# Start of a one-core transformer block: inputs laid out in tile order, shift, scale and first GLU products block by block

## The chip, the cores and the metric

The kernel runs on one core of a Trainium2 chip. TensorE (PE) multiplies matrices and loads its stationary operand beside that (PEld), VectorE (DVE) and ScalarE (ACT) work on whole tiles, GpSimd (POOL) does the same more slowly, and SyncE (SP) issues nearly all DMAs, which 16 DMA engines carry out. The metric is the device time of one execution in microseconds. Host work that prepares the inputs is outside it, in both kernels.

## The reference, cut to what matters

The block takes 256 latent tokens `x` and 256 context tokens `ctx` of 1024 channels and two condition vectors `c` and `c_ctx`. It begins so:

```python
mod_lat = silu(c)     @ w_ada + b_ada        # 6 x 1024 columns: shift, scale, gate, twice
mod_ctx = silu(c_ctx) @ w_ada + b_ada
u_ctx = h_ctx * (1 + csc_m) + csh_m          # per channel
u_lat = h_lat * (1 + sc_m) + sh_m
q, k, v, g, glu, gates = split(u_lat @ w_in + b_in)      # w_in: 1024 x 10240
k_c, v_c = split(u_ctx @ w_in[:, K_OFF:G_OFF] + b_in[K_OFF:G_OFF])
za, zb = split(glu); z = za * sigmoid(zb)    # then a depthwise convolution, 31 taps per channel
```

After that come retention over q, k and v, the convolution branch, two gated output projections, a layer norm, a router that picks two of 32 experts per token, the experts' SwiGLU products (6 MB of float32 weights each) and a second layer norm.

## The kernel before

All of it is one program on one core, in float32. The products of the mixing stage are made three times at reduced precision: each operand is split into a high and a low part, and `mm3` (line 96) adds high by high, high by low and low by high. The split of a weight slice (128 x 1024) is one copy on ACT and one subtraction on VectorE (`Slice.emit`, lines 163 and 164); that of the input is in `modulate` (line 293), per block of 128 channels: the high part on ACT, the full value and the low part on VectorE.

What comes first is written out by hand. Lines 371 to 387 load `w_ada` in pieces of 512 rows x 512 columns (`ada_load`, 1 MB each, rows of 2 KB), multiply them with the condition vectors (`ada_half`), copy the sums out (`ada_row`), and transpose them into columns of shift and scale (`ada_mod`). Column block 2 (scale) comes first and block 0 (shift) second; these two cover channels 0 to 511. Between them the program loads parameters as rows of 128 numbers and turns them into columns by PE transposes (`load_cond`, `params`, `more_params`), and transposes x, 16 times 128 x 128 (`transpose_in`, line 284). The decay rates of the retention are computed here as well (`decay_rates`, line 248).

Then `early` (line 483) runs: six clock fillers (`keep_clock`: matmuls whose result nobody reads), the modulation of channels 0 to 511, and GLU products. GLU has four column groups `hb` of 512 columns, and each has four slices `kq` of 256 input channels. `early` does slices 0 and 1 of groups 0 to 2, with column blocks 3 and 1 of `w_ada` between them, and then modulates channels 512 to 1023. Two matmuls with a zero operand open the accumulators of each group (line 435).

The other slices are steps in a list that `run_steps` (line 192) works off: a step emits the splits of up to two later slices (`LEAD`), does its matmuls, its post-processing, and pops `NTAP` operations of the depthwise convolution for VectorE. `ctx` is loaded and transposed on PE, and modulated by steps placed by `CTX`; the sections of `w_ada` that are used later come as side operations from step `SIDE0` on (`ada_rest`, line 784). After the GLU steps come `distances`, the k, q, v and g projections (`proj_k`, line 555, and others), retention, the gates and output projections. A step list sets the order on all engines; SyncE issues loads in program order, each when a buffer of its tag is free (`W8` four, `Y8` six, `Q8` three).

The expert stage (from line 1587) goes through 16 pairs of experts. `load_to` (line 1040) issues each weight tile, 1 MB with rows of 8 KB, as soon as the buffer that `slots` names is free. The `down` weights of the last pair are loaded in column pieces (`load_cols_of`, line 1035).

Of the kernel before, what the change touches and what calls it, by code (L numbers as in the profile page):

```python
# [17 lines left out]
D = 1024  # L18
NT = 256
# [10 lines left out]
SIDE0, SIDE = 4, 9  # L30
NPOS, APOS, TPOS, QPOS, AHEAD = 7, 9, 7, 5, ()
NTAP = (3, 5, 3, 4, 4, 2)
KS0, KS1 = 6, 0
# [4 lines left out]
CTX = 2, 6, 7, 8, 2  # L38
EB = (0, 0), (1, 0), 9
# [6 lines left out]
def tile_block(ctx, tc, a, out):  # L46
# [9 lines left out]
    w_in = a["w_in"][0]  # L56
    w_ada = a["w_ada"][0]
# [187 lines left out]
    for i, nm in enumerate(("ret_decay_fwd", "ret_decay_bwd")):  # L245
        gload(lgx[:, 8 * i:8 * i + 8], bass.AP(tensor=a[nm].tensor, offset=a[nm].offset, ap=[[0, P], [1, 8]]))
# [17 lines left out]
    V.memset(s32, 0.0)  # L264

    def load_cond():
        rows = row1("crow2", (16, P))
        load(rows[0:8], a["c"].rearrange("o (r c) -> (o r) c", c=P))
        load(rows[8:16], a["c_ctx"].rearrange("(r c) -> r c", c=P))
        S.activation(rows, rows, AF.Silu)  # L270
        ps = misc("pps")
        T.transpose(ps[:, 0:16], rows, ident[:16, :16])
        V.tensor_copy(pcol[:, 0:16], ps[:, 0:16])
        V.tensor_copy(s32[:, :, 0], pcol[:, 0:8])
        V.tensor_copy(s32[:, :, 1], pcol[:, 8:16])

    def load_params():
        rows = row1("prow", (48, P))
        load(rows[0:16], a["b_ada"][0, 0:2048].rearrange("(r c) -> r c", c=P))
        for i, nm in enumerate(("conv_dw_b", "conv_ln_g", "conv_ln_b", "b_conv_out")):  # L280
            load(rows[16 + 8 * i:24 + 8 * i], a[nm][0].rearrange("(r c) -> r c", c=P))
        return rows

    def transpose_in(src, dst, name):
        for k2 in range(4):
            ps = misc(f"{name}{k2}", (P, 2, NT))
            for kk in range(2):
                for t in range(2):
                    T.transpose(ps[:, kk, t * P:(t + 1) * P],
                                src[:, t, (2 * k2 + kk) * P:(2 * k2 + kk + 1) * P], ident)  # L290
            S.activation(dst[:, 2 * k2:2 * k2 + 2, :], ps, AF.Copy)
# [12 lines left out]
    def load_tok(name):  # L304
        t = big("Y8", [P, 2, D], f"{name}_t")
        load(t, a[name][0].rearrange("(t p) d -> p t d", p=P))
        return t

# [3 lines left out]
    brow = row1("brow", (80, P))  # L312
    crow = big("Y8", [TAPS, D], "crow")
# [5 lines left out]
    def ada_load(cb, r):  # L319
        adas["w", cb, r] = load_rows(w_ada, 512 * r, 512 * cb, f"wa{cb}_{r}")  # L320

    def ada_half(cb, r):
        if r == 0:
            adas[cb] = acc(f"ada{cb}")
        ps, w = adas[cb], adas["w", cb, r]
        for j in range(4):
            T.matmul(ps[32 * j:32 * j + 32, :], s32[:, 4 * r + j, :], w[:, j, :],
                     start=(r == 0), stop=(r == 1))

    def ada_row(cb):  # L330
        row = adas["r", cb] = sb.tile([P, 512], F32, tag="b2", name=f"adr{cb}", bufs=2)
        S.activation(row, adas[cb], AF.Copy)

    def ada_mod(cb):
        row = adas["r", cb]
        pt = misc(f"adt{cb}", (P, 4, P))
        for c in range(4):
            T.transpose(pt[:, c, :], row[:, c * P:(c + 1) * P], ident)
        m = mod[:, :, 4 * cb:4 * cb + 4]
        V.tensor_reduce(m.rearrange("p r c -> p c r"), pt.rearrange("p c (j r) -> p c r j", r=32)[:, :, 0:2, :],  # L340
                        op=ALU.add, axis=AX.X)
        for r in range(2):
            V.scalar_tensor_tensor(m[:, r], m[:, r], 1.0 if cb >= 2 else 0.0, pcol[:, 16 + 4 * cb:20 + 4 * cb],
                                   op0=ALU.add, op1=ALU.add)

    start = {}

    def load_rest():
        start["p"], start["x"] = load_params(), load_tok("x")

    def params():
        ps = misc("pps2")
        T.transpose(ps[:, 0:48], start["p"], ident[:48, :48])
        V.tensor_copy(pcol[:, 16:64], ps[:, 0:48])

    def load_rest2():
        load(brow, a["b_in"][0].rearrange("(r c) -> r c", c=P))
        load(crow, a["conv_dw"][0])
        transpose_in(start["x"], xT, "xt")

    def more_params(_):
        ps = misc("pbs")
        T.transpose(ps[:, 0:80], brow, ident[:80, :80])
        V.tensor_copy(bcol, ps[:, 0:80])
        ps = misc("pts", (P, 8, 32))
        for k in range(8):
            T.transpose(ps[:, k, 0:TAPS], crow[:, k * P:(k + 1) * P], ident[:TAPS, :TAPS])
        V.tensor_copy(taps, ps[:, :, 0:TAPS])


    ada_load(2, 0)
    load_cond()
    ada_half(2, 0)
    ada_load(2, 1)
    decay_rates()
    load_rest()
    ada_half(2, 1)
    ada_row(2)
    params()
    ada_mod(2)  # L380
    ada_load(0, 0)
    load_rest2()
    ada_half(0, 0)
    ada_load(0, 1)
    ada_half(0, 1)
    ada_row(0)
    ada_mod(0)
# [29 lines left out]
    def load_glu(hb, r):  # L417
        t = big("W8", [P, 4, 512], f"wz{hb}_{r}")
        for h in range(2):
            c0 = GLU_OFF + D * h + 256 * hb  # L420
            load(t[:, :, 256 * h:256 * h + 256],
                 w_in[512 * r:512 * r + 512, c0:c0 + 256].rearrange("(k p) c -> p k c", p=P))
        return t

    gws, gsl, gmm = {}, {}, {}

    def glu(hb):
        ws = gws[hb] = [lazy(load_glu, hb, r) for r in range(2)]
        box = {}

        def mm(kq, q, between=None):
            if kq == 0:
                for i in range(2):
                    box[i] = (misc if hb == 2 else acc)(f"glu{2 * hb + i}", (P, 2, NT))
                    T.matmul(box[i], zero, ulat[0][0:1, 0:2, :], start=True, stop=False)
            for i in range(2):
                for h in range(2):
                    if between and (i, h) in between:
                        between[(i, h)]()
                    cs = slice(256 * h + P * i, 256 * h + P * i + P)  # L440
                    for kk in range(2):
                        k = 2 * kq + kk
                        mm3(box[i][:, h], (q[0][:, kk, cs], q[1][:, kk, cs]), (ulat[0][:, k, :], ulat[1][:, k, :]),
                            False, k == 7 and h == 1)
# [10 lines left out]
        def steps_(kqs):  # L455
            for kq in kqs:
                step(lambda q, kq=kq: mm(kq, q), post if kq == 3 else None, sl[kq], NTAP[0])
                yield

        sl = gsl[hb] = [Slice(lambda kq=kq: ws[kq // 2]()[:, 2 * (kq % 2):2 * (kq % 2) + 2, :], f"qz{hb}_{kq}")  # L460
                        for kq in range(4)]
        gmm[hb] = lambda kq, between=None: mm(kq, sl[kq].q, between)
        return steps_(range(4) if hb > 2 else (2, 3))
# [3 lines left out]
    def ctx_load(_):  # L467
        cbox["t"] = load_tok("ctx")

    def ctx_tr(_):  # L470
        cbox["T"] = big("X8", [P, 8, NT], "cT")
        transpose_in(cbox["t"], cbox["T"], "ct")
# [10 lines left out]
    def early():  # L483
        more_params(None)
        keep_clock(KS0)
        gsl[0][0].emit()
        gws[1][0]()
        ada_load(3, 0)
        ada_load(3, 1)
        modulate(xT, ulat, 0, 0, 4, "um")  # L490
        gsl[0][1].emit()
        gmm[0](0)
        gsl[1][0].emit()
        gws[2][0]()
        gmm[0](1)
        ada_load(1, 0)
        ada_half(3, 0)
        ada_half(3, 1)
        gsl[1][1].emit()
        ada_row(3)  # L500
        ada_load(1, 1)
        gws[0][1]()
        gws[1][1]()
        gmm[1](0)
        ada_mod(3)
        gsl[2][0].emit()
        gmm[1](1)
        gsl[2][1].emit()
        ada_half(1, 0)
        gmm[2](0, {EB[0]: lambda: (ada_half(1, 1), ada_row(1)), EB[1]: lambda: ada_mod(1)})  # L510
        gmm[2](1, {EB[2]: lambda: ada_mod(1)})
        keep_clock(KS1)
        gsl[0][2].emit()
        modulate(xT, ulat, 0, 4, 6, "um")
        modulate(xT, ulat, 0, 6, 8, "um")
# [1180 lines left out]
```

## Time and profile before

| | us |
|---|---|
| median of 3 runs | 996.86 (996.44 to 998.81) |
| the profiled execution, its own time | 1000.41 |
| its span in the profile | 998.6 |
| PE busy | 942.7 |
| VectorE busy | 506.3 |
| ACT busy | 310.2 |
| GpSimd busy | 104.4 |
| DMA moved | 294.81 MB, 295 GB/s on average |

Times in the profile count from the start of the span. A busy PE is not a PE at its peak: matmuls are pipelined, and the clock that the chip grants TensorE has two levels, 1.2 and 2.4 GHz; the profile shows the granted clock as a share, 0.50 or 1.00, with a mean where a window holds both. Up to the first change that the profile records, a window shows 1.00 whatever the clock was. In a row of the timeline the duration runs from the start of the first instruction to the end of the last of those merged into it; one float32 matmul leaves two records.

### The profile page before, as it was taken

The numbers are of one execution on the slowest core, as the hardware profiler recorded it, in microseconds if no ns is written. First come the engines' busy times: TensorE is split into PE (matmuls) and PEld (weight loads), VectorE is DVE, ScalarE is ACT, GpSimd is POOL, SyncE is SP. The second block draws the span as 40 slices with busy tenths as digits, with TensorE's granted clock in tenths as the row PEclk, the third lists the DMA queues.
The fourth block names the chain that finished last, engine by engine and source line by source line (L and its number), as shares of the span: only waits on it lengthen the run. The fifth ranks groups of instructions, "written<-read, shape, count | busy, mean of one in ns | idle before, by whom it ended". The sixth has DMA issues, their size and how long they took to land. (4 is left out here: it accounts for less than half of the span.)

```text
span 998.6 us, 15317 instructions
## 1 busy us (share of the span) xinstructions
PE 942.7 (94%) x6354; PEld 691.5 (69%) x6354; DVE 506.3 (51%) x976; ACT 310.2 (31%) x458; POOL 104.4 (10%) x122
## 2 busy tenths in 40 slices
PE   3999999999999999989989999999999989999884
PEld 2799879779879869889976655656565554655452
DVE  1377988897886996785884111222221111222135
ACT  3357735443543444375443111111110101111010
POOL 1002120210210020721520000000000000000001
PEclk9699999999999999999999999999999998999998
DMA  8795634544374347759986899999999999999991
GB/s 269 231 362 202 220 107 129 214 143 160 115 253 142 136 139 239 268 185 289 348 331 272 346 419 419 421 420 420 420 419 420 421 419 421 421 420 420 421 366 44
DMA packets 92424, 294.81 MB, mean 295 GB/s; under 512 B 6921, under 2 KB 37825, under 8 KB 68288
## 3 DMA queue, kind: packets, MB, share of 16 engines
q1 hardware_dynamic: 91360, 293.31, 76.4%
q0 software_dynamic: 992, 0.49, 0.4%
q8 instruction: 51, 0.84, 0.4%
q14 instruction: 21, 0.17, 0.1%
HBM read 292.71 MB, written 1.06 MB: 294 GB/s over the span
## 5 line engine op out<-in xcount | busy, mean ns | idle before, releaser
L1465 PE MATMUL dn<-wdown,hT 128*64 128x512 f32 (+1 forms) x528 | 120.7, 584 | 6.3 <-DMA wdown<-in_w_exp_down_dram 6.0
L1365 PE MATMUL gu<-wgate,xe 128*64 128x256 f32 x1024 | 122.5, 391 | 2.2 <-DVEq L1625 2.2
L1365 PE MATMUL gu<-wup,xe 128*64 128x256 f32 x1024 | 118.3, 380 | 4.2 <-DMA wup<-in_w_exp_up_dram 4.1
L1371 DVE TENSOR_TENSOR h<-h,gu 128x256 f32<-128x256 f32 x32 | 13.5, 421 | 198.2 <-ACT h L1370 198.2
L404 DVE SCALAR_TENSOR_TENSOR slab<-zp,taps,slab 128x256 f32<-128x256 f32 x232 | 107.1, 515 | 0.0
L1365 PEld LDWEIGHTS gu<-wgate,xe 128*64 128x64 f32 x1024 | 74.5, 141 | 45.8 <-issue 10.3
L1365 PEld LDWEIGHTS gu<-wup,xe 128*64 128x64 f32 x1024 | 74.1, 137 | 42.8 <-DMA wup<-in_w_exp_up_dram 8.2
L1465 PEld LDWEIGHTS dn<-wdown,hT 128*64 128x64 f32 x528 | 37.6, 136 | 76.6 <-issue 59.9
L1370 ACT ACTIVATE h<-gu 128x256 f32<-128x256 f32 x32 | 12.3, 385 | 210.9 <-PE gu L1365 210.8
L1480 DVE SCALAR_TENSOR_TENSOR dl<-dn,ws,ohq 128x512 fp32r<-128x512 f32 x30 | 22.5, 751 | 104.3 <-ACT ohq L1479 104.3
L1479 ACT ACTIVATE ohq<-dn,ws 128x512 fp32r<-128x512 f32 x30 | 20.6, 688 | 125.4 <-PE dn L1465 122.7
L98 PE MATMUL ya<-rT,qro 128*128 128x256 f32 x128 | 36.7, 286 | 2.6 <-DVE rT L750 2.6
L97 PE MATMUL glu<-ulh,qz 128*128 128x256 f32 x128 | 37.5, 293 | 0.0
L99 PE MATMUL ya<-rT,qro 128*128 128x256 f32 x128 | 36.6, 286 | 0.8 <-DVE qro L164 0.8
L97 PE MATMUL ya<-rT,qro 128*128 128x256 f32 x128 | 36.9, 288 | 0.0
L99 PE MATMUL gt<-ulh,qg 128*128 128x256 f32 x128 | 35.8, 280 | 1.1 <-DVE qg L164 1.1
L98 PE MATMUL glu<-ull,qz 128*128 128x256 f32 x128 | 36.8, 287 | 0.0
L99 PE MATMUL glu<-ulh,qz 128*128 128x256 f32 x128 | 36.7, 287 | 0.0
L97 PE MATMUL gt<-ulh,qg 128*128 128x256 f32 x128 | 36.6, 286 | 0.0
L1358 ACT ACTIVATE xe<-ga,cf 128x256 f32<-128x256 f32 x36 | 19.8, 564 | 52.5 <-PE ga L1351 52.5
L98 PE MATMUL gt<-ull,qg 128*128 128x256 f32 x128 | 35.8, 279 | 0.0
L1351 PE MATMUL ga<-ohq,xnh 128*128 128x256 f32 x112 | 30.4, 306 | 0.0
(477 smaller groups left out, 2159.1 us busy)
## 6 DMA issues: line engine op xcount, KB each, us to landing
wgate<-in_w_exp_gate_dram SPq DMA_DIRECT2D x64, 1024.0 KB, 19.8
wup<-in_w_exp_up_dram SPq DMA_DIRECT2D x64, 1024.0 KB
wdown<-in_w_exp_down_dram SPq DMA_DIRECT2D x60, 1024.0 KB, 19.8
wa<-in_w_ada_dram SPq DMA_DIRECT2D x24, 1024.0 KB, 9.4
wz<-in_w_in_dram SPq DMA_DIRECT2D x16, 512.0 KB, 7.5
wro<-in_w_ret_out_dram SPq DMA_DIRECT2D x8, 1024.0 KB
wg<-in_w_in_dram SPq DMA_DIRECT2D x8, 1024.0 KB, 9.9
wk<-in_w_in_dram SPq DMA_DIRECT2D x4, 1024.0 KB, 12.3
```

The lines of the kernel that those rows point to most:

```text
L97: T.matmul(ps, st[0], mv[0], start=start, stop=False)
L98: T.matmul(ps, st[0], mv[1], start=False, stop=False)
L99: T.matmul(ps, st[1], mv[0], start=False, stop=stop)
L404: V.scalar_tensor_tensor(dst, zp[:, ct, j:j + NT], taps[:, ct, j:j + 1], ac[ct], op0=ALU.mult, op1=ALU.add)
L1351: T.matmul(ps[:, kk], xns[s][:, t, k // 4, k % 4], ohr[:, t], start=(i == 0), stop=(i == 3))
L1358: S.activation(xe[c][:, k], ps[:, kk], AF.Identity, scale=fsc[:, k:k + 1], bias=fsh[:, k:k + 1])
L1365: T.matmul(ps[64 * hf:64 * hf + 64, j], xe[c][:, k, CAP * i:CAP * i + CAP], w[:, k % 4, NT * hf:NT * hf + NT], start=start, stop=stop)
L1370: S.activation(h, ps[:, 0], AF.Silu)
L1371: V.tensor_mul(h, h, ps[:, 1])
L1465: T.matmul(ps[64 * x:64 * x + 64], hT[x][:, ch % 2, 64 * (ch // 2):64 * (ch // 2) + 64], w, start=(ch == 0), stop=(ch == 3))
L1479: S.activation(dh, ps, AF.Copy, scale=ws)
L1480: V.scalar_tensor_tensor(dl, ps, ws, dh.bitcast(F32), op0=ALU.mult, op1=ALU.subtract)
```

## The change

Numpy prepares the weights of `w_ada`, `w_in`, `w_ret_out`, `w_conv_out` and `w_mix_out` so that every tile lies in memory partition by partition: what came to a partition as four rows of 2 KB, or eight of 1 KB, is one contiguous row of 8 KB (4 KB for half a GLU tile, 2 KB for each channel pair of x). `x` and `ctx` come transposed, and the small parameters as columns in one array, `col_params`. On the chip the transposes for them are gone.

`w_ada`'s shift and scale columns are reordered: block k holds the 128 shift columns and the 128 scale columns of channel block k (1024 x 256, 1 MB). `early` now loads block 0, x, a half of a GLU tile and so on in the order written, and for each k makes shift and scale, modulates channel block k, and lets the GLU products of that block follow. GLU products are called per channel block (12 products) instead of per slice (24). `early` now covers slices 0 to 2 of groups 0 and 1 and slices 0 and 1 of group 2; the remaining eight slices are steps. The accumulators' openers use a constant instead of the modulated input and are issued first. The decay rates move into the step `distances`; a convolution tap more is popped per GLU step; `CTX` and `SIDE0` follow the smaller number of steps. The last expert pair's `down` tiles come as one 1 MB piece each, then two pieces of 512 KB each, in rows of 8 and 4 KB. The arithmetic is that of before.

```diff
-SIDE0, SIDE = 4, 9
+SIDE0, SIDE = 2, 9
-NTAP = (3, 5, 3, 4, 4, 2)
-KS0, KS1 = 6, 0
+NTAP = (4, 5, 3, 4, 4, 2)
+KS = 8, 4, 4
-CTX = 2, 6, 7, 8, 2
-EB = (0, 0), (1, 0), 9
+CTX = 0, 0, 5, 6, 2
...
-    def load_cols(w, c0, name):
+    def load_cols(w, i, name):
         t = big("W8", [P, 8, 256], name)
-        load(t, w[:, c0:c0 + 256].rearrange("(k p) c -> p k c", p=P))
+        load(t, w[i].rearrange("p (k c) -> p k c", k=8))
...
-    def load_rows(w, r0, c0, name, tag="W8"):
+    def load_rows(w, r, i, name, tag="W8"):
         t = big(tag, [P, 4, 512], name)
-        load(t, w[r0:r0 + 512, c0:c0 + 512].rearrange("(k p) c -> p k c", p=P))
+        load(t, w[r, i].rearrange("p (k c) -> p k c", k=4))
...
-    def load_cond():
-        rows = row1("crow2", (16, P))
...
-    def load_params():
...
-    def transpose_in(src, dst, name):
...
+    load(pcol, a["col_params"][:, 0:64])
+
+    S.activation(l1[:, 0:1], onef[:, 0:1], AF.Silu)
+
+    def cond():
+        S.activation(pcol[:, 0:16], pcol[:, 0:16], AF.Silu)
+        for r in range(2):
+            V.tensor_copy(s32[:, :, r], pcol[:, 8 * r:8 * r + 8])
+        V.tensor_scalar(pcol[:, 24:32], pcol[:, 24:32], 1.0, None, op0=ALU.add)
...
+    def ada_load(k):
+
+        w = adas["w", k] = big("Y8", [P, 8, 256], f"wa{k}")
+        load(w, a["w_ada_m"][k].rearrange("p (k c) -> p k c", k=8))
+
+    def ada_mm(k):
+
+        ps = acc(f"ada{k}")
+        for j in range(8):
+            b = 32 * (j % 4)
+            T.matmul(ps[b:b + 32, 0:256], s32[:, j, :], adas["w", k][:, j, :], start=(j < 4), stop=(j >= 4))
+        row = adas["r", k] = sb.tile([P, 256], F32, tag="b2", name=f"adr{k}", bufs=2)
+        S.activation(row, ps[:, 0:256], AF.Copy)
+
+    def ada_mod(k):
+        pt = misc(f"adt{k}", (P, 2, P))
+        for c in range(2):
+            T.transpose(pt[:, c, :], adas["r", k][:, c * P:(c + 1) * P], ident)
+        m = mod.rearrange("p r (c k) -> p k c r", c=2)[:, k]
+        V.tensor_reduce(m, pt.rearrange("p c (j r) -> p c r j", r=32)[:, :, 0:2, :], op=ALU.add, axis=AX.X)
+        V.tensor_add(m, m, bc(pcol[:, 16:32].rearrange("p (c k) -> p k c", c=2)[:, k, :, None], (2, 2)))
+        modulate(xT, ulat, 0, k, k + 1, "um")
...
+        def mm(k, q):
+            if not box:
+                zeros()
+            kk = k % 2
             for i in range(2):
                 for h in range(2):
...
+                    mm3(box[i][:, h], (q[0][:, kk, cs], q[1][:, kk, cs]), (ulat[0][:, k, :], ulat[1][:, k, :]),
+                        False, k == 7 and h == 1)
...
     def early():
-        more_params(None)
-        keep_clock(KS0)
+
+        ada_load(0)
+        load_x(xT, "xT", 0, 2)
+        glu_tile(0, 0)
+        load_glu(0, 0, 0, 1)
+        gload(bcol, a["col_params"][:, 64:144])
+        gload(taps, a["col_params"][:, 144:392].rearrange("p (k j) -> p k j", k=8))
+        gload(lgx, a["col_params"][:, 392:408])
+        ada_load(1)
...
+        ada_load(5)
+        keep_clock(KS[0])
+        for hb in range(3):
+            gz[hb]()
+        cond()
+        ada_mm(0)
+        keep_clock(KS[1])
+        ada_mod(0)
         gsl[0][0].emit()
...
+        keep_clock(KS[2])
+        ada_mm(1)
+        gmm[0](0)
+        ada_mod(1)
+        ada_load(6)
+        glu_tile(0, 1)
+        load_glu(0, 1)
+        ada_load(7)
+        gsl[1][0].emit()
+        gmm[0](1)
+        gsl[2][0].emit()
+        gmm[1](0)
+        ada_mm(2)
+        gmm[1](1)
+        ada_mod(2)
...
-    takes = [0] * 2 + [1] * 2 + [2] * 2 + [3] * 4
+    takes = [0, 1] + [2] * 2 + [3] * 4
...
     def distances(_):
+        decay_rates()
         gload(rope, a["rope_tab"])
...
-    def load_cols_of(which, c0, n):
-        for t, src, d0 in which:
-            for h in range(2):
-                load(t[:, 2 * h:2 * h + 2, c0:c0 + n], src[h][:, :, d0 + c0:d0 + c0 + n])
+    def load_piece(which, o, n):
+        for e, t in which:
+            load(t.rearrange("p k f -> p (k f)")[:, o % 2048:o % 2048 + n], a["w_down_last"][e - (NE - 2), :, o:o + n])
```

## Rows read from the trace of the kernel before

**Rows 1.** Page, part 1: engine, busy us (share of the span), instructions
```profile
PE 942.7 (94%) x6354; PEld 691.5 (69%) x6354; DVE 506.3 (51%) x976; ACT 310.2 (31%) x458; POOL 104.4 (10%) x122
```

**Rows 2.** PE's timeline (start, duration, what); last row: k products, first to last start
```profile
8.04 0.28 PE L272 MATMUL pps<-ident,crow 16*128 16x16 f32 x1 [8.04 <-ACT crow L270]
12.74 1.93 PE L327 MATMUL ada<-wa,s 128*32 128x512 f32 x8 [1.93 <-DMA wa<-in_w_ada_dram]
31.27 2.93 PE L106 MATMUL clk<-oner,ident 128*128 128x128 f32 x12
35.28 0.58 PE L97 MATMUL glu<-ulh,qz 128*128 128x256 f32 x1
L97 PE MATMUL kp<-ulh,qwk x64: 277/280/468, 93.6 to 317.7; 128*128 128x256 f32 x64
```

**Rows 3.** Windows: length; busy of PE, PEld, DVE, ACT, POOL; granted clock; DMA; GB/s
```profile
35.28:93.60 58.32, 58.32 (x464) 52.09 (x463) 39.11 (x66) 29.12 (x42) 3.68 (x4) 0.96 0.76 254
35.28:40.35 5.07, 5.07 (x24) 5.07 (x24) 3.23 (x5) 0.00 (x0) 0.00 (x0) 0.50 0.36 117
```

**Rows 4.** Waits of PE, 40 to 150 us: total, times, longest
```profile
PE adb L807 <- DMA adr<-in_b_ada_dram: 0.3, 1, 0.3
```

**Rows 5.** Windows as in rows 3, and issues in SyncE's timeline
```profile
0.00:2.00 2.00, 0.00 (x0) 0.00 (x0) 0.81 (x4) 0.00 (x0) 1.35 (x12) 1.00 0.05 9
4.00:6.00 2.00, 0.00 (x0) 0.00 (x0) 0.00 (x0) 0.00 (x0) 0.00 (x0) 1.00 1.17 361
550.00:555.00 5.00, 5.00 (x26) 1.66 (x24) 0.75 (x1) 0.69 (x1) 0.00 (x0) 1.00 0.29 84
600.00:620.00 20.00, 20.00 (x152) 11.27 (x152) 4.29 (x10) 2.33 (x4) 0.00 (x0) 1.00 1.01 420
...
0.74 0.44 SPq L75 DMA_DIRECT2D wa<-in_w_ada_dram  x1
...
553.42 2.03 SPq L75 DMA_DIRECT2D wup<-in_w_exp_up_dram  x2
```

**Rows 6.** One tile's windows (glu, ada, ct); then PE's timeline: transposes, openers
```profile
35.28:93.60 58.32, 50.96 (x391) 48.51 (x390) 3.53 (x8) 3.75 (x8) 0.96 0.76 254
35.28:93.60 58.32, 4.05 (x32) 0.73 (x32) 1.20 (x2) 0.96 0.76 254
35.28:93.60 58.32, 1.95 (x16) 1.75 (x16) 2.07 (x4) 0.96 0.76 254
...
48.86 0.60 PE L338 MATMUL adt<-ident,adr 128*128 128x128 f32 x4
...
77.88 0.73 PE L435 MATMUL glu<-ulh,zero 1*128 1x512 f32 x2
```

**Rows 7.** Groups, 0 to 70 us: busy us, mean ns of one, idle before and releaser
```profile
L163 ACT ACTIVATE qz<-wz 128x1024 fp32r<-128x1024 f32 x12 | 12.6, 1054 | 12.2 <-PE glu L99 11.1 <-ACT qz L163 0.8 <-DMA wz<-in_w_in_dram 0.3
L164 DVE TENSOR_TENSOR qz<-wz,qz 128x1024 fp32r<-128x1024 f32 x11 | 13.2, 1220 | 3.9 <-ACT qz L163 3.6 <-issue 0.3
L297 ACT ACTIVATE ulh<-xT,mod 128x256 fp32r<-128x256 f32 x8 | 4.2, 590 | 1.2 <-DVE mod L343 1.2
L302 DVE TENSOR_TENSOR ull<-um,ulh 128x256 fp32r<-128x256 f32 x8 | 3.4, 426 | 0.8
L332 ACT ACTIVATE adr<-ada 128x512 f32<-128x512 f32 x4 | 2.4, 598 | 17.6 <-PE ada L327 17.6
L340 DVE TENSOR_REDUCE mod<-adt 128x8 f32<-128x32 f32 x4 | 0.8, 193 | 25.8 <-PE adt L338 25.8
L270 ACT ACT_TABLE_LOAD x1 | 1.3, 1283 | 6.4 <-DMA crow<-in_c_ctx_dram 6.4
```

**Rows 8.** VectorE's timeline: sigmoid step, three conv taps alone, three beside GpSimd
```profile
66.87 0.91 DVE L451 SCALAR_TENSOR_TENSOR zp<-glu,bcol,sgz 128x256 f32<-128x256 f32 x2 [0.56 <-ACT sgz L450]
69.87 1.28 DVE L404 SCALAR_TENSOR_TENSOR slab<-zp,taps,slab 128x256 f32<-128x256 f32 x3
86.27 2.27 DVE L404 SCALAR_TENSOR_TENSOR slab<-zp,taps,slab 128x256 f32<-128x256 f32 x3
```

More of the change, by code (lines that the diff above doesn't have):

```diff
@@ L317, in tile_block @@
     adas = {}
[L319 to L368, printed above, removed]
@@ L414, in conv_pair, with glu_tile, load_glu, zeros @@
             conv_ops.append(lambda: G.tensor_add(csum, csum, zc[:, c0 + 1]))
-    def load_glu(hb, r):
-        t = big("W8", [P, 4, 512], f"wz{hb}_{r}")
-        for h in range(2):
[L420 to L425, printed above, removed]
+    def glu_tile(hb, r):
+        gws[hb, r] = big("W8", [P, 4, 512], f"wz{hb}_{r}")
+    def load_glu(hb, r, i0=0, i1=2):
+        load(gws[hb, r][:, 2 * i0:2 * i1],
+             a["w_glu"][hb, r][:, 1024 * i0:1024 * i1].rearrange("p (k c) -> p k c", c=512))
+    gws, gsl, gmm, gz = {}, {}, {}, {}
     def glu(hb):
-        ws = gws[hb] = [lazy(load_glu, hb, r) for r in range(2)]
         box = {}
[L431 to L435, printed above, removed]
+        def zeros():
+            for i in range(2):
+                box[i] = (misc if hb == 2 else acc)(f"glu{2 * hb + i}", (P, 2, NT))
+                T.matmul(box[i], zero, oner[0:1, None, :].to_broadcast([1, 4, P]), start=True, stop=False)
+        gz[hb] = zeros
+        def mm(k, q):
+            if not box:
+                zeros()
+            kk = k % 2
             for i in range(2):
                 for h in range(2):
-                    if between and (i, h) in between:
-                        between[(i, h)]()
                     cs = slice(256 * h + P * i, 256 * h + P * i + P)
[L441 to L444, printed above, removed]
+                    mm3(box[i][:, h], (q[0][:, kk, cs], q[1][:, kk, cs]), (ulat[0][:, k, :], ulat[1][:, k, :]),
+                        False, k == 7 and h == 1)
         def post():
@@ L456, in steps_, with both, source @@
             for kq in kqs:
-                step(lambda q, kq=kq: mm(kq, q), post if kq == 3 else None, sl[kq], NTAP[0])
+                def both(q, kq=kq):
+                    mm(2 * kq, q)
+                    mm(2 * kq + 1, q)
+                step(both, post if kq == 3 else None, sl[kq], NTAP[0])
                 yield
[L460 to L463, printed above, removed]
+        def source(kq):
+            if (hb, kq // 2) not in gws:
+                glu_tile(hb, kq // 2)
+                load_glu(hb, kq // 2)
+            return gws[hb, kq // 2][:, 2 * (kq % 2):2 * (kq % 2) + 2, :]
+        sl = gsl[hb] = [Slice(lambda kq=kq: source(kq), f"qz{hb}_{kq}") for kq in range(4)]
+        gmm[hb] = lambda k: mm(k, sl[k // 2].q)
+        return steps_({0: (3,), 1: (3,), 2: (2, 3), 3: range(4)}[hb])
     cbox = {}
     def ctx_load(_):
-        cbox["t"] = load_tok("ctx")
-    def ctx_tr(_):
         cbox["T"] = big("X8", [P, 8, NT], "cT")
-        transpose_in(cbox["t"], cbox["T"], "ct")
+        load_x(cbox["T"], "ctxT", 0, 8)
     def ctx_mod(k):
@@ new lines, in early @@
+        gload(bcol, a["col_params"][:, 64:144])
+        gload(taps, a["col_params"][:, 144:392].rearrange("p (k j) -> p k j", k=8))
+        gload(lgx, a["col_params"][:, 392:408])
+        ada_load(1)
+        glu_tile(1, 0)
+        load_glu(1, 0, 0, 1)
+        glu_tile(2, 0)
+        load_glu(2, 0, 0, 1)
+        ada_load(2)
+        load_x(xT, "xT", 2, 4)
+        ada_load(3)
+        for hb in range(3):
+            load_glu(hb, 0, 1, 2)
+        ada_load(4)
+        load_x(xT, "xT", 4, 8)
@@ new lines, in early @@
+        ada_load(5)
+        keep_clock(KS[0])
+        for hb in range(3):
+            gz[hb]()
[3 more added lines that the diff above has]
+        ada_mod(0)
+        gsl[0][0].emit()
+        keep_clock(KS[2])
[12 more added lines that the diff above has]
+        gmm[1](1)
@@ new lines, in early @@
+        ada_mod(2)
+        gsl[0][1].emit()
+        gmm[2](0)
+        ada_mm(3)
+        gmm[2](1)
+        ada_mod(3)
+        gsl[1][1].emit()
+        gmm[0](2)
+        gmm[0](3)
+        gsl[2][1].emit()
+        ada_mm(4)
+        gmm[1](2)
+        ada_mod(4)
+        ada_mm(5)
+        gmm[1](3)
+        ada_mod(5)
+        gsl[0][2].emit()
+        gmm[2](2)
+        ada_mm(6)
+        gmm[2](3)
+        ada_mod(6)
+        gsl[1][2].emit()
+        gmm[0](4)
+        ada_mm(7)
+        gmm[0](5)
@@ L595, in proj_n @@
     def proj_n(c0, acts, emit, name, ntap):
-        ws = [lazy(load_rows, w_in, 512 * r, c0, f"{name}w{r}") for r in range(2)]
+        ws = [lazy(load_rows, a["w_vg"], r, (c0 - V_OFF) // 512, f"{name}w{r}") for r in range(2)]
         box = {}
@@ L754, in ret_out @@
     def ret_out(p):
-        ws = [lazy(load_rows, a["w_ret_out"][0], 512 * p, 512 * ch, f"wro{p}_{ch}") for ch in range(2)]
+        ws = [lazy(load_rows, a["w_ret_out"], p, ch, f"wro{p}_{ch}") for ch in range(2)]
         for i in range(4):
@@ L1461, in product @@
                     if last:
-                        w = wts[e0 + x, "down", cb][:, ch, cs]
+                        w = wts[e0 + x, "down", cb]
+                        w = w[:, cs.start // 256, ch] if cb else w[:, ch, cs]
                     else:
@@ L1682 @@
     nc = bacc.Bacc("TRN2", target_bir_lowering=False, num_devices=1)
+    inputs = {name: np.asarray(x) for name, x in inputs.items()}
     feed = {name: np.ascontiguousarray(inputs[name]) for name in _INS}
     feed.update(constants())
+    feed.update(layouts(inputs))
     arrays, args = {}, {}
```

143 lines of the change are left out of this document (54 added, 89 removed).

## The prediction

> **What bounds the kernel now.** I read the page first: TensorE (PE) is busy for 942.7 us of a span of 998.6 [rows 1], so all its idle time is 56 us, and the question is where that lies. The timeline of PE shows its first instruction at 8.04 us, released late, and the first GLU product only at 35.28; the tile view of the k projection puts its first product at 93.6 [rows 2]. Between these two PE has no gap: 58.32 us busy of 58.32, though the first 5.07 of them ran at a granted clock of 0.50, the lower level of 1.2 GHz [rows 3]. From 40 to 150 us PE waits for a DMA for 0.3 us in all [rows 4]; later weight loads of the mixing stage are not on the path.
>
> At the other end the DMA engines are the bound: 420 GB/s without a break in the expert stage. But that stream is continuous only from about 555: between 550 and 555 it moves 84 GB/s, because SyncE waits for a weight buffer that PE's expert products release, and issues again at 553.42 [rows 5]. What is left to load then is the same in both kernels, so the end follows PE's progress up to 553, and a microsecond gained before the k projection is a microsecond at the end. That is the lever; the rest of the change can add or lose little.
>
> **The start, step by step.** Removed ahead of the first product: the row loads and transposes that make the parameter columns and xT, and the need for all of shifts and scales of half the channels. In their place one 1.05 MB block of weights gives shift and scale of 128 channels, and two of eight channel blocks are enough to begin.
>
> Loads. The first bytes move after 2 us (0 to 2 shows 9 GB/s). The new rows are 4 to 8 KB instead of 1 to 2 KB; the rate lies between 361 GB/s (4 to 6 us, 2 KB rows) and 420 (the expert stage, 8 KB rows) [rows 5]. Columns, block 0, the first x and GLU pieces are 1.87 MB: moved by 2 + 4.5 to 5.2 = 6.5 to 7.2 us, in use some 1.5 us later. (An estimate: ACT waited to 6.39 for the rows of c behind the first 1.05 MB [rows 7], where 2 us and 1.05 MB at 361 GB/s make 4.9.) SyncE has 16 issues before its first wait, at 0.44 us each [rows 5]: faster than the data. GpSimd's three parameter loads are needed only at the first sigmoid.
>
> PE meanwhile. Eight clock fillers need only the identity and start near 2.2 us. At the lower clock six cost 2.93 us [rows 2] (the row counts each in two records), so eight cost 3.9. Six accumulator openers follow at 0.73 us a pair [rows 6], twice that when slow: 2.2 to 4.4. That makes 8.3 to 10.5 us, by which the first data are there. The first matrix-vector block then costs 1.0 to 1.9: the fast price is half of a 512-column block (two such cost 4.05 [rows 6]), the slow one is the 1.93 of a row of the same work [rows 2]. Then a chain that nothing covers: four fillers of 0.25 to 0.49 us, under which ACT copies the row (0.60); two transposes, 0.3 to 0.6; the reduction and the addition on VectorE, 0.19 each (the addition taken like the reduction); the high half of the modulation, 0.59; the copy of the weight slice, 1.05; its low half, 1.22 [rows 6, 7]. Together 4.7 to 6.0. So products run freely from 14.0 to 18.4; I take **16.2**, the middle.
>
> From there to the k projection. Before: 58.32. Away go the 16 ctx transposes, 1.95 [rows 6], two pairs of openers (moved under the loads), 1.4, and the slow clock on 24 products: 5.07 against 24 x 0.12 = 2.9 (the rest of the glu row, 50.96 less 5.07, over its other 367 records is 0.125) [rows 3, 6], so 2.2. To it come the matrix-vector blocks that now run behind the first product: seven of eight instead of two of four, 1.5 x 2.03 = 3.0, and six more transposes, 0.60 for four, 0.9 [rows 6]. 58.32 - 1.95 - 1.4 - 2.2 + 3.0 + 0.9 = **56.7**, if PE never waits.
>
> It will wait somewhere. Each of the seven later blocks hands over PE, ACT, PE, VectorE, ACT, VectorE: copy 0.6, transposes 0.3, two small operations 0.4, modulation 0.59 + 0.43, about 2.3 us, in queues that also split weight slices (1.05 and 1.22) [rows 7]. PE has one group of 12 products (1.4 us) and the next block's 1.0 to cover it, 2.4. Even: I allow 2.5 us in all, bounds 0 and 7 (1 us a block). Bytes do not set it: 17.8 MB of weights and x take 42 to 49 us at these rates, against 57 of products; blocks 6 and 7 and the second GLU pieces may come 1 or 2 us late, which is inside that bound. After the stream there are four conv taps a step instead of three. Three taps take 1.27 us, and 2.27 when GpSimd works beside them [rows 8]. A step is then 1.22 + 1.7 = 2.9 us of VectorE against 24 x 0.12 = 2.9 of PE, with 0.91 more at each sigmoid step [rows 8]: I allow 1, bounds 0 and 4.
>
> So the k projection starts at 16.2 + 56.7 + 2.5 + 1 = **76.4** instead of 93.6: 17.2 us earlier.
>
> **The rest of the change.** Decay rates move behind the GLU stage: ten small VectorE operations and two activations with a table load each of 1.28 us [rows 7], in ACT's queue ahead of the slices of q. Two k projections of 48 products, 5.7 us each, cover it; taken as 0, bounds 0 and 3. Ctx comes transposed, so ACT loses four copies. The loads of the later weights in 8 KB rows: 0, since PE waits for none [rows 4]; without that cover they would gain, by 361 against 420 GB/s [rows 5]. The last expert pair's pieces: 0, because the DMA-bound stretch ends with weights that stand before them in the queue; bounds 0 and a gain of 2.
>
> Sum: 996.86 - 17.2 = **979.7 us**. The profiled execution took 1000.41 (span 998.6), 3.6 above the median, and goes by the same sum to 983; the forecast is made against the median.
>
> **Rivals.** *The clock falls in the stream.* The profile of before shows the price: after idling, PE needed 24 products at 0.21 us instead of 0.12 before its clock rose [rows 3]. The Trainium skill ("TensorE: Matmul & The Clock Gate", section "HAM oscillation — how this bites in real kernels") warns that short groups of matmuls with waits between them throttle the array again each time; the trace agrees as far as one such idle stretch goes. In this kernel 16 groups of 12 products and seven blocks lie in the streamed part. At the lower clock throughout they cost 192 x 0.09 = 17.3 and 7 x 0.95 = 6.7, together 24 us: the k projection at 100.4, 6.8 later than before, and the time **1003.7**, the one case that ends slower. It turns slower once 17.2 / 24 = 72% of the streamed part runs slow. Against it: fillers stand in the first two gaps, and the later gaps are below 1 us by the sum. For a third to two thirds of it (8 to 16 us lost): 988 to 996.
>
> *Handoffs or loads hold PE at every block.* The upper bounds of the stalls, 7 + 4 instead of 3.5, and 18.4 instead of 16.2: 9.7 more, **989**.
>
> *The gain is hidden anyway*, if the expert stream did not wait for PE. Then the end is that of the stream, **996.9**. Against it stands the hole of 84 GB/s before 555 [rows 5].
>
> *It goes better than costed:* first product at 14.0 and no stalls: 5.7 less, **974**; with a gain of 2 at the tail 972.
>
> **How the numbers follow.** Forecast (975 to 984) 0.66; better 0.12; held at every block or part of the stream slow (984 to 996) 0.16; slow throughout 0.03; hidden 0.03. A change under 0.3%, 3 us, can't be told from none. Faster by more: 0.66 + 0.12 + 0.15 = 0.93; same 0.04; slower 0.03. The range, 972 to 988, leaves out some 0.04 below and, of the slow, the hidden and the worst held cases, 0.12 above.
>
> **What would show it.** First GLU product near 14 to 18 us, first k product near 76, granted clock 1.00 from there; PE's waits for wa and wz below a microsecond each; the hole in the expert stream near 535. A first k product beyond 85, or a clock of 0.50 between 15 and 50, makes the forecast wrong; so does a k projection near 76 with an unchanged end.

## The result, and the profile after

The changed kernel takes 982.1 us (981.03 to 984.44, 4 runs) against 997.84 for the kernel before in the same comparison: a ratio of 0.9846, interval 0.9823 to 0.987. That is faster by 15.7 us; the forecast was 17.2 us and 979.7, with a range of 972 to 988. In a later comparison the same kernel took 981.21 against 999.27, a ratio of 0.982 (0.9795 to 0.9844). One execution among all the runs below, the profiled one of ah_again, took 1566.66 us at a mean granted clock of 0.56 and is left out of the times.

The page's first part shows what answers to [rows 1]: PE is busy for 6.0 us less, and its share of the span goes from 94% to 96%.

```profile
PE 936.7 (96%) x6395; PEld 688.7 (70%) x6395; DVE 507.5 (52%) x977; ACT 306.7 (31%) x455; POOL 108.5 (11%) x123
```

The timeline of PE, from its first instruction to the second product (start, duration, what, idle time before):

```profile
2.15 3.78 PE L103 MATMUL clk<-oner,ident 128*128 128x128 f32 x16 [2.15 <-DVE oner L222]
5.87 2.92 PE L358 MATMUL glu<-oner,zero 1*128 1x512 f32 x6
8.72 1.94 PE L302 MATMUL ada<-wa,s 128*32 128x256 f32 x16
10.59 2.08 PE L103 MATMUL clk<-oner,ident 128*128 128x128 f32 x8
12.81 0.66 PE L309 MATMUL adt<-ident,adr 128*128 128x128 f32 x2
13.74 2.08 PE L103 MATMUL clk<-oner,ident 128*128 128x128 f32 x8 [0.27 <-DVE mod L311]
15.74 1.93 PE L302 MATMUL ada<-wa,s 128*32 128x256 f32 x16
17.60 0.38 PE L94 MATMUL glu<-ulh,qz 128*128 128x256 f32 x1
17.83 0.28 PE L95 MATMUL glu<-ull,qz 128*128 128x256 f32 x1
```

The first product comes at 17.60 instead of 35.28 [rows 2]. Everything ahead of it ran at the lower clock: a shift and scale block took 1.93, and the same work 1.07 in another profile below. From 17.60 the products follow each other at the fast pitch, 0.11 to 0.12 us.

The windows with the columns of [rows 3], the waits of PE up to 80 us, the tile view of the k projection, and the windows of one tile (glu, then ada):

```profile
8.00:17.60 9.60, 9.18 (x52) 5.12 (x51) 2.40 (x5) 1.93 (x3) 0.00 (x0) 1.00 1.03 418
17.60:76.90 59.30, 57.81 (x516) 50.40 (x512) 42.32 (x78) 32.35 (x48) 5.09 (x4) 1.00 0.78 314
```

```profile
PE clk L103 <- DVE oner L222: 2.2, 1, 2.2
PE glu L94 <- ACT ulh L274: 1.1, 1, 1.1
PE glu L96 <- DVE qz L161: 0.3, 1, 0.3
PE clk L103 <- DVE mod L311: 0.3, 1, 0.3
```

```profile
L94 PE MATMUL kp<-ulh,qwk x64: 277/280/468, 76.9 to 302.1; 128*128 128x256 f32 x64
```

```profile
17.60:76.90 59.30, 50.01 (x386) 46.33 (x386) 2.73 (x6) 3.81 (x8) 1.00 0.78 314
17.60:76.90 59.30, 6.50 (x100) 2.50 (x96) 2.69 (x7) 1.00 0.78 314
```

The first k product stands at 76.9 against 93.6 [rows 2]: 16.7 us earlier. In the streamed part PE waits for no transfer at all, once 1.1 us for ACT's high half of the second channel block and once 0.3 for a weight slice. The window's clock of 1.00 proves nothing by itself, since it stands over the slow blocks ahead of 17.60 too; the products do: none of the 384 took more than 0.39 us, where those at the lower clock before took 0.41 and more. So the streamed part ran at the higher clock throughout, where [rows 3] begins with 5.07 us at 0.50. Up to 17.60 the DMA engines move 418 GB/s, and PE waits for none of it: the rows of 4 and 8 KB keep pace.

At the other end, SyncE's timeline and two windows of the changed kernel around the hole in the expert stream, for [rows 5]:

```profile
524.66 3.78 SPq L72 DMA_DIRECT2D wgate<-in_w_exp_gate_dram  x2
535.78 2.03 SPq L72 DMA_DIRECT2D wup<-in_w_exp_up_dram  x2
```

```profile
530.00:535.00 5.00, 5.00 (x27) 1.96 (x27) 1.26 (x5) 0.69 (x1) 0.00 (x0) 1.00 0.72 300
600.00:620.00 20.00, 20.00 (x138) 12.04 (x136) 5.14 (x11) 3.46 (x6) 0.00 (x0) 1.00 1.01 420
```

SyncE issues again at 535.78 instead of 553.42, 17.6 us earlier, and the stream then runs at 420 GB/s as before. What was gained by 76.9 arrives there whole, and nothing between takes it back.

### The profile page after: what moved, and what is told of

Read it like the earlier page. It is cut to its first block, busy times and chain, and to the rows that moved or that the text cites. A ratio compares the mean times of both kernels' runs of the same rounds, so it can differ in the third digit from the quotient of the medians.

```text
span 979.9 us, 15383 instructions
## 1 busy us (share of the span) xinstructions
PE 936.7 (96%) x6395; PEld 688.7 (70%) x6395; DVE 507.5 (52%) x977; ACT 306.7 (31%) x455; POOL 108.5 (11%) x123
## 3 DMA queue, kind: packets, MB, share of 16 engines
HBM read 292.71 MB, written 1.06 MB: 300 GB/s over the span
## 5 line engine op out<-in xcount | busy, mean ns | idle before, releaser
L1437 PEld LDWEIGHTS dn<-wdown,hT 128*64 128x64 f32 x528 | 37.4, 137 | 76.7 <-issue 60.3
## 6 DMA issues: line engine op xcount, KB each, us to landing
wa<-in_w_ada_m_dram SPq DMA_DIRECT2D x8, 1024.0 KB, 14.4
```

Of the source, the lines that this page charges most:

```text
L1437: T.matmul(ps[64 * x:64 * x + 64], hT[x][:, ch % 2, 64 * (ch // 2):64 * (ch // 2) + 64], w, start=(ch == 0), stop=(ch == 3))
```

## The experiments

The change does three things at once: it lays out weights in rows as long as a tile's, it brings x, ctx and the parameters as columns, and it makes the first products channel block by channel block. The runs take these apart. In one comparison the kernel before runs beside each; its median was 1000.25 beside the first four below, 999.27 beside the next four and 999.73 beside the last three. Times are medians; the two starts are those of the one execution that was profiled:

| run | median us | ratio (interval) | first GLU product | first k product |
|---|---|---|---|---|
| before | 997.84 to 1000.25 | 1 | 35.28 | 93.6 |
| a_weights | 998.9 | 0.9984 (0.9966 to 1.0003) | 36.8 | 94.6 |
| h_columns | 989.71 | 0.9911 (0.9882 to 0.9941) | 26.2 | 82.4 |
| ah_layout | 985.81 | 0.9875 (0.9844 to 0.9906) | 24.9 | 79.4 |
| b_strided | 990.48 | 0.9914 (0.9883 to 0.9945) | 17.3 | 83.6 |
| t_split | 991.85 | 0.9916 (0.9887 to 0.9944) | 26.88 | 85.3 |
| after_again | 981.21 | 0.982 (0.9795 to 0.9844) | 13.19 | 72.5 |
| ah_again | 986.2 | 0.9874 (0.985 to 0.9897) | | |
| d_nofill | 981.85 | 0.9822 (0.9799 to 0.9845) | 14.22 | 75.0 |
| i_rows31 | 988.04 | 0.9897 (0.9877 to 0.9917) | 19.64 | 79.7 |
| i_rows16 | 982.66 | 0.982 (0.9797 to 0.9843) | 17.41 | 76.7 |
| f_taps | 982.46 | 0.9836 (0.9813 to 0.986) | 17.6 | 77.2 |

### The weights alone (a_weights)

The kernel before, with its loads of weights taken from tile-ordered arrays, each tile one row per partition, and nothing else:

```diff
...
-        load(t, w[r0:r0 + 512, c0:c0 + 512].rearrange("(k p) c -> p k c", p=P))
+        load(t, w[r, i].rearrange("p (k c) -> p k c", k=4))
...
```

> Kernel before with only the weights of w_ada, w_in, w_ret_out, w_conv_out and w_mix_out in contiguous tiles, order as before. Theory (loads were the longest link of the old start: PE waited 5.5 us for wa before 26.45 and its clock then fell): the first GLU product comes at 25 to 29 us instead of 35.28, the first k product at 82 to 86, the time is 7 to 11 us below before. Rival (the order by channel blocks gives the gain, the rate of the loads little): first product at 33 to 35, time 0 to 3 us below before.

It was worth nothing that can be told: 998.9, and a first product at 36.8. The theory, 7 to 11 us and a first product at 25 to 29, was wrong. PE still waits 7.0 us for one piece of `w_ada`, whose block starts at 27.97 (26.45 before). The windows of that stretch show the DMA engines first full with what stands behind the piece, then nearly idle (last two columns: their busy share and GB/s):

```profile
24.00:26.00 2.00, 0.00 (x0) 0.00 (x0) 0.00 (x0) 0.00 (x0) 0.00 (x0) 0.50 0.96 369
26.00:28.00 2.00, 0.03 (x4) 0.03 (x5) 0.00 (x0) 0.00 (x0) 0.00 (x0) 0.50 0.35 143
28.00:30.00 2.00, 1.90 (x8) 0.17 (x8) 0.00 (x0) 0.03 (x1) 0.00 (x0) 0.50 0.07 29
```

A busy share of 0.07 is about one engine of the 16 (1/16 = 0.0625): when the piece is there at last, all but about one engine have nothing left to do. The rate of the 16 together was not what the old start waited for.

### The columns alone (h_columns), and both layouts (ah_layout)

The kernel before, with x, ctx and the parameters loaded as columns and the transposes gone; the weights and the order are the old ones. ah_layout adds the weights of a_weights.

```diff
...
-        load(brow, a["b_in"][0].rearrange("(r c) -> r c", c=P))
-        load(crow, a["conv_dw"][0])
-        transpose_in(start["x"], xT, "xt")
+        load(bcol, a["col_params"][:, 64:144])
+        load(taps, a["col_params"][:, 144:392].rearrange("p (k j) -> p k j", k=8))
...
```

> Kernel before with only x, ctx and the small parameters taken as transposed columns, weights and order as before. Theory: the removed PE transposes that lay on the path are those of ctx (1.95 us) and of the parameters behind the second block (1.4); the x transposes lay beside a wait for wa. 2 to 5 us below before. Rival (row loads and transposes held the chain): 6 us or more below before.

> Both of the two edits above on the kernel before: everything laid out, nothing streamed by channel blocks. Theory: about the sum of both, 10 to 14 us below before, so that 2 to 6 of the 16 us are left to the new order; first GLU product 22 to 27 us. Rival (the order carries it): less than 6 us below before.

The columns gave 10.5 us (1000.25 - 989.71), more than twice the 5 that I expected at most, and the two layouts together 14.4. So the weights' layout, worth nothing alone, seems to be worth some 4 us on top of the columns; the intervals of these two overlap, so its size is loose. PE's waits for `w_ada` fall from 7.5 us to 4.5 and 3.8, each of them below 2 us. The long wait was gone with the columns, but none of the transposes or small loads that I had counted costs 10 us.

What the 4 us are is open. The first k products stand 3.0 us apart (82.4 and 79.4), of which the shorter waits for `w_ada` make 0.7. For most of the rest, h_columns runs its first 20 or so GLU products at the lower clock (0.21 us each) and ah_layout none of them. No run shows that the layout is what raises the clock sooner, and below the same kernel does it at two different times. The profiled execution of ah_layout, 980.86, is also the fastest of the ten of this kernel: it takes 431.9 us from the first k product to the first expert product, where the other eleven profiles take 434.3 to 436.2. Its start goes with the median, its end does not.

### One load of 31 rows (t_split)

The trace of the kernel before holds a suspect. Its timeline of SyncE, and of PE where it waits longest:

```profile
13.09 0.28 SPq L75 DMA_DIRECT2D crow<-in_conv_dw_dram  x1
13.42 0.39 SPq L75 DMA_DIRECT2D wa<-in_w_ada_dram  x1
```

```profile
26.45 1.93 PE L327 MATMUL ada<-wa,s 128*32 128x512 f32 x8 [5.52 <-DMA wa<-in_w_ada_dram]
```

While PE waits, the DMA engines of the kernel before move less than they can (columns of [rows 3]):

```profile
22.00:24.00 2.00, 0.00 (x0) 0.00 (x0) 0.00 (x0) 0.00 (x0) 0.00 (x0) 0.84 0.46 134
24.00:26.00 2.00, 0.00 (x0) 0.00 (x0) 0.00 (x0) 0.00 (x0) 0.00 (x0) 0.50 0.89 283
26.00:28.00 2.00, 1.54 (x8) 0.20 (x8) 0.00 (x0) 0.00 (x0) 0.00 (x0) 0.50 0.88 265
```

The convolution's taps (`crow`, 31 rows of 4 KB, 124 KB) are loaded just ahead of the last piece of `w_ada` that the first products need. The run issues the same rows in two loads and changes nothing else:

```diff
-        load(crow, a["conv_dw"][0])
+        load(crow[0:16], a["conv_dw"][0, 0:16])
+        load(crow[16:TAPS], a["conv_dw"][0, 16:TAPS])
```

> Kernel before with one edit: the load of conv_dw, 31 rows of 4 KB, is issued as 16 and 15 rows. New theory (a load of 31 rows goes over one of the 16 DMA engines, 124 KB at a sixteenth of 420 GB/s is 4.7 us, and the next w_ada piece has its share queued behind it on that engine): PE's wait for wa before 26.45 us falls from 5.5 to under 2 us, first GLU product at 28 to 32 us instead of 35.28, first k product at 85 to 91 instead of 93.6, time 3 to 9 us below before. Rival (the wait comes from the number of loads or bytes ahead of that piece): PE waits as long, time within 1.5 us of before.

991.85 against 999.27: 7.4 us by one line. The timeline of PE in t_split:

```profile
18.75 1.07 PE L327 MATMUL ada<-wa,s 128*32 128x512 f32 x8
21.15 1.06 PE L327 MATMUL ada<-wa,s 128*32 128x512 f32 x8 [1.34 <-DMA wa<-in_w_ada_dram]
...
26.88 0.38 PE L97 MATMUL glu<-ulh,qz 128*128 128x256 f32 x1
```

The wait of 5.52 is 1.34, the block behind it runs at the faster clock (1.06 instead of 1.93), and the first product comes 8.4 us earlier, more than I expected (28 to 32). Only half of that is the wait itself, 4.2 us. Another 3.1 come behind it: from this block to the first product PE needs 5.73 us instead of 8.83, at the higher clock that it lost in the long wait before (0.50 from 24 us on). And 1.1 stand ahead of it, the block before at 18.75 instead of 19.85. An estimate from the rows fits: 124 KB over one engine at 420/16 = 26 GB/s take 4.8 us. The Trainium skill ("DMA: Bandwidth & Descriptors", section "🔬 Why a DMA increments its semaphore by 16 and not by 1") states how this comes about: a transfer goes over the largest number of engines, up to 16, that divides its outer dimension, and 31 is prime. The traces agree as far as they show it: the share of 0.07 above, and the two runs that come next.

### The same load put into the changed kernel (i_rows31, i_rows16)

The converse: the changed kernel with 124 KB more at the head of its stream, once as 31 rows in one load, once as 16 and 15.

```diff
     def early():
+        held = slab.rearrange("p k n -> p (k n)")
+        load(held[0:31, 0:1024], a["w_ada_m"][7, 0:31, 0:1024])
         ada_load(0)
```

> The changed kernel with one transfer more at the head of its stream, whose data nobody reads: 31 rows of 4 KB (127 KB). It is the converse of the run that issued the old 31-row load in two parts. Theory (a load of 31 rows goes over one of 16 engines, some 4.7 us, and every later transfer waits for its sixteenth part behind it): block 0 of the shift and scale weights, in place at 6.5 us without fillers, and block 1, at 12.2, land 4 to 5 us later; the first product comes at 17 to 20, PE waits for wa several us, and the time is 2 to 5 above the changed kernel's 981.2: 983 to 986. Rival (127 KB are 0.3 us of the 16 engines, whichever rows they come in): 981 to 982.5.

> The same transfer with the same bytes, issued as 16 and 15 rows. Theory: blocks 0 and 1 land within 1 us of the changed kernel's, time 981 to 982.5, at least 2 below the run with 31 rows in one. Rival (the loss, if there is one, comes from the place in the queue or from small rows): the same time as with 31 rows in one.

988.04 and 982.66, and the intervals of the ratios don't touch. The loss of 5.4 us puts 988.04 above the range of the theory (983 to 986); with the rows split it is nothing that can be told. The timeline of PE and the DMA issues of the first 14 us (KB each, median us from issue to landing) in i_rows31, then the issues in i_rows16:

```profile
12.78 1.93 PE L302 MATMUL ada<-wa,s 128*32 128x256 f32 x16 [4.96 <-DMA wa<-in_w_ada_m_dram]
```

```profile
wa<-in_w_ada_m_dram SPq DMA_DIRECT2D x4, 1024.0 KB, 13.4
slab<-in_w_ada_m_dram SPq DMA_DIRECT2D x1, 124.0 KB
```

```profile
wa<-in_w_ada_m_dram SPq DMA_DIRECT2D x4, 1024.0 KB, 10.9
slab<-in_w_ada_m_dram SPq DMA_DIRECT2D x1, 64.0 KB, 2.4
slab<-in_w_ada_m_dram SPq DMA_DIRECT2D x1, 60.0 KB, 2.2
```

PE waits 4.96 us for the first block of weights that was issued behind the 31 rows, and the blocks take 13.4 us to land instead of 10.9. The parts of 16 and 15 rows are there in 2.4 and 2.2. The two profiled executions, 984.60 and 984.80, show no difference at their end, though the first k product stands 3.0 us apart (79.7 and 76.7): the profiled one was the fastest of six of i_rows31 and the slowest of five of i_rows16. The medians are what tells the two apart, not these two executions.

### The order without the layout (b_strided)

The changed kernel, with the weights of its first stretch taken from the old arrays: shift and scale blocks in rows of 512 bytes, GLU tiles in rows of 1 KB.

```diff
-        load(w, a["w_ada_m"][k].rearrange("p (k c) -> p k c", k=8))
+        for h in range(2):
+            load(w[:, :, P * h:P * h + P], a["w_ada"][0][:, D * h + P * k:D * h + P * k + P].rearrange("(k p) c -> p k c", p=P))
...
```

> Changed kernel, but the w_ada blocks of the stream and the GLU weights are loaded from the old arrays in rows of 512 B and 1 KB; order, columns and later weights as changed. Theory (the stream needs the rate): the loads run at 200 to 300 GB/s in the first 50 us, PE waits for wa and wz for several us in all, first k product at 83 to 95 instead of 76.9, time 988 to 1000. Rival (the chain PE, ACT, VectorE sets the pace, the loads are hidden): first k product 77 to 79, time 982 to 985.

990.48: about half of the gain is lost. Windows of b_strided, then of the changed kernel, with the columns of [rows 3]:

```profile
20.00:30.00 10.00, 9.61 (x89) 7.83 (x90) 4.27 (x9) 4.46 (x7) 0.00 (x0) 1.00 1.10 318
35.00:40.00 5.00, 2.90 (x32) 2.19 (x34) 1.59 (x5) 0.98 (x2) 0.00 (x0) 1.00 1.13 302
40.00:45.00 5.00, 5.00 (x37) 4.38 (x38) 0.48 (x3) 0.53 (x2) 0.00 (x0) 0.66 1.10 322
```

```profile
20.00:30.00 10.00, 9.34 (x87) 7.54 (x88) 5.23 (x9) 4.75 (x7) 0.00 (x0) 1.00 1.03 418
35.00:40.00 5.00, 5.00 (x53) 3.91 (x46) 1.86 (x5) 1.37 (x3) 0.00 (x0) 1.00 1.01 415
40.00:45.00 5.00, 5.00 (x51) 4.28 (x50) 3.02 (x8) 2.21 (x4) 0.00 (x0) 1.00 1.01 421
```

The engines show a busy share of 1.10 to 1.13, no lower than in the changed kernel (1.01 to 1.03), yet move 302 to 322 GB/s instead of 415 to 421. PE starts as early (17.3), but from 35 to 40 it is busy for 2.90 of 5 us, among the rest with 2.0 us of waiting for a block of `w_ada`, and then its granted clock falls to a mean of 0.66. The streamed order starts PE so early that the loads become the bound; the long rows lift it.

### The order on top of the layout (after_again, ah_again)

> The changed kernel, for comparison with the layout alone on the same chip. Theory (the new order is worth what the first k product shows, 79.4 less 76.9): 1.5 to 4 us below the layout alone. Rival (that lead is given back later): within 1 us of it.

> Kernel before with everything laid out and nothing streamed, again. Theory: 1.5 to 4 us above the changed kernel. Rival: within 1 us of it.

981.21 and 986.2: what is left of the change once both layouts are there is worth 5.0 us (5.4 by the ratios), more than I expected; the intervals of the ratios do not touch. Beside the order by channel blocks this holds the openers issued first, the fillers, the fourth tap, the moved decay rates and the pieces in which the last expert pair's `down` weights come. The fillers and the tap are worth nothing that can be told (below), and the pieces nothing that shows (after the next rows); the decay rates and openers were not run apart from the order. ah_again is ah_layout once more, for its time alone; the starts of this kernel are those of ah_layout.

The profile of after_again shows how far one start differs from another. It is the same kernel, and these are the instructions of the timeline under the result:

```profile
5.79 1.65 PE L358 MATMUL glu<-oner,zero 1*128 1x512 f32 x6
7.37 1.07 PE L302 MATMUL ada<-wa,s 128*32 128x256 f32 x16
...
13.19 0.39 PE L94 MATMUL glu<-ulh,qz 128*128 128x256 f32 x1
```

Here the clock rose during the openers, near 6 us, and not at 17.6. The first product comes 4.4 us earlier, the first k product too (72.5), but the profiled executions took 980.67 and 982.01: 1.3 us are left of it at the end. Of the 4.4 us, 1.3 are gone by the release of the expert stream (532.66 here, 535.78 there), by what I did not settle. The rest goes near the end. Windows of the changed kernel's profile, then of after_again:

```profile
920.00:930.00 10.00, 8.05 (x39) 3.27 (x40) 2.13 (x6) 0.69 (x1) 0.00 (x0) 1.00 1.01 419
920.00:930.00 10.00, 8.03 (x28) 2.22 (x24) 0.75 (x1) 0.69 (x1) 0.00 (x0) 0.83 1.01 418
```

In after_again the granted clock falls once more here, some 50 us before the end (0.83 in the second row). Six of the twelve profiles (that of ah_again left aside) show such a fall between 920 and 960, and they take 469.3 to 470.2 us from the first expert product to the end; the six without it take 467.8 to 468.5. Kernels with the old and with the new pieces of the last pair stand in both groups: the fall goes with some 1.4 us, and the pieces with nothing that shows. That the fall costs them is not shown, only that the two go together. Single executions, then, tell nothing apart below some 2 us.

### The fillers and the fourth tap (d_nofill, f_taps)

The changed kernel without any clock fillers (`KS = 0, 0, 0`), and with three convolution taps a step as before (`NTAP = (3, 5, 3, 4, 4, 2)`).

> Changed kernel without its 16 clock fillers in the start. Theory A (the fillers hold the clock up): the first GLU products run at the lower clock, 0.21 us each, for 5 us or more, and the first k product comes at 78 to 84; 1 to 6 us above the changed kernel. Theory B (the fillers ran at the lower clock themselves and only take PE's time): first GLU product at 13 to 15 us instead of 17.6, first k product at 73 to 76, 1 to 4 us below the changed kernel.

> The changed kernel with three convolution taps a GLU step as before, not four. The prediction charged the fourth tap 1 us, bounds 0 and 4. Theory (VectorE has slack in these steps, PE waits for nothing of it): the first k product within 1 us of the changed kernel's, time 980 to 982.5. Rival 1 (the taps hold the weight slices up): first k product and time 2 to 4 lower, 977 to 979. Rival 2 (the taps that are not done then are late afterwards): the time 2 or more higher, 983 and up.

Neither is told apart from the changed kernel. Without fillers the starts are those of theory B, but the time that either theory forecast, above or below, did not come: 981.85 against 981.21. The first product comes at 14.22 and the first twelve run at the lower clock; PE waits 3.9 us for two blocks of weights. The timeline of d_nofill:

```profile
6.51 1.93 PE L302 MATMUL ada<-wa,s 128*32 128x256 f32 x16 [1.18 <-DMA wa<-in_w_ada_m_dram]
12.35 1.93 PE L302 MATMUL ada<-wa,s 128*32 128x256 f32 x16 [2.73 <-DMA wa<-in_w_ada_m_dram]
14.22 0.58 PE L94 MATMUL glu<-ulh,qz 128*128 128x256 f32 x1
```

The first k product is at 75.0, between the two profiles of the kernel with fillers (72.5 and 76.9). With three taps it is at 77.2, and PE's waits up to 80 us are those of the changed kernel, row for row. The fourth tap costs nothing that can be told.

## Why the prediction was right, point by point

**What bounds, and the lever: right.** The forecast said that a microsecond gained ahead of the k projection is one at the end. Across the runs, the first k product and the median moved together: 8.3 and 7.4 us (t_split), 11.2 and 10.5 (h_columns), 10.0 and 9.8 (b_strided), 16.7 and 15.7 for the change itself. In all eleven, the change and the ten of the table with a start, they agree within 3.0 us; the worst is after_again, 21.1 and 18.1. Finer than that the rule does not hold: after_again's start is the one of the rival "better than costed" (974), and its time is not. The rival "hidden" is out: the release of the expert stream moved by 17.6.

**First product at 16.2 (14.0 to 18.4): 17.60 and 13.19 in two profiles.** The second lies outside the range. The terms held at the lower clock: eight fillers took 3.78 (3.9 forecast) and the openers 2.92 (2.2 to 4.4). One thing was missed: the second block of weights is multiplied ahead of the first product, not behind it, 1.1 to 1.9 us that the start did not count and that the part behind had too many. From the end of the first block to the first product it was 7.0 us at the lower clock and 4.8 at the higher, where 4.7 to 6.0 were forecast (the terms listed add up to 4.5 to 5.8). SyncE waited after nine issues, not sixteen (from 5.42 to 6.32), without cost: PE waited for no transfer. I had the clock rise by the fillers; in one profile they ran at the lower clock to the end, in the other it rose after the first eight.

**From there 56.7 + 3.5 us: measured 59.30**, of them 57.81 busy. That 56.7 came so near is luck in part: it has one block too many, 1.0 us, and the products cost 0.130 us a record (50.01 over 386) instead of the 0.125 taken, some 1.9 us more. PE waited 1.4 us where 2.5 were allowed for the handoffs. The allowance for the fourth tap, 1, was not needed (f_taps), and the clock stayed at its higher level. So the rivals "the clock falls" (1003.7) and "handoffs or loads hold PE" (989) did not come about, but b_strided shows that they were near: with rows of 512 bytes and 1 KB both set in, at 990.48.

**The k projection at 76.4: 76.9. The rest at 0: right.** The nearness is luck as well: 1.4 us more than forecast at the start, 0.9 less behind it, and another execution stood at 72.5. Between the k projection and the expert stage the lead changes from 16.7 to 17.7 us (first expert product at 511.4 against 529.1), which is within what profiles of one kernel differ by. The decay rates and the later weights take and give nothing that shows; a_weights says the same of the weights for the whole kernel.

**What I did not see** is what held the old start. "Removed ahead of the first product: the row loads and transposes" names it as a sum of small things and prices the new start only, so the difference came out right without its cause. The largest part of the cause was one load: 7.4 us, of the 15.7 to 18.1 that the change gains, are given by two lines for one in the kernel before. The row that told it was there: a wait of 5.52 us for a piece of 1 MB that was issued at 13.42 and used at 26.45, while the windows from 22 to 28 us (shown with t_split) moved 134 to 283 GB/s, not 360 to 420. I read the start of the new kernel from rows and the start of the old one from its code.

Adding up, from 999.27 to 981.21: 7.4 for the load of 31 rows; up to 3 for the other row loads and transposes (h_columns against t_split, 10.5 and 7.4; the ratios, 0.9911 and 0.9916, don't tell them apart); some 4 with the weights' rows, how much of it by the clock is open; 5.0 for the order by blocks and what goes with it. That makes 16.4 to 19.4 against 18.1 measured; the terms come from different comparisons. The order needs the rows: without them PE starts at 17.3 and reaches the k projection at 83.6.

## What to carry to other kernels

Before pricing a new start, find what ends the last wait of the old one: for a large piece whose bytes should long have come, look at the small loads issued just ahead of it. Give loads a number of rows that spreads over the DMA engines (here 16 and 15 instead of 31), above all those that stand ahead of something urgent. A stream of loads in long rows is worth nothing while something else holds PE, and is what an earlier start of PE then stands on: measure such parts together as well as alone. A wait can cost twice, once in itself and once by the clock that falls in it: here 4.2 and 3.1 us.

## What the runs showed of the hardware that was not expected

- 124 KB in 31 rows cost 7.4 us in one kernel (991.85 against 999.27) and 5.4 in another (982.66 against 988.04), compared with the same rows as 16 and 15; in the second kernel the parts landed in 2.4 and 2.2 us.
- With eight fillers from 2.15 us on, the granted clock of the same kernel rose near 6 us in one execution and at 17.6 in another, PE being busy in both. Without fillers, and with idle time of 1.2 to 2.7 us between, products were fast from about 18.7. The times of these three executions lie within 1.4 us (980.67 to 982.01).
- Rows of 512 bytes and 1 KB kept the DMA engines at a busy share of 1.1 and moved 302 to 322 GB/s; rows of 4 and 8 KB moved 415 to 421 at 1.01 to 1.03.
- A fall of the granted clock (a mean of 0.83 over 10 us) some 50 us before the end goes with 1.4 us: six profiles with it, six without.
